# Wider fill beside the attention of a hybrid block, and four of its gates moved into the dense stage

## The chip, the cores and the metric

The kernel runs on one core of a Trainium2 chip. The metric is the device time of one execution in microseconds (us). A core has five engines with their own instruction queues: TensorE (PE, matrix products and transposes), VectorE (DVE), ScalarE (ACT), GpSimd (POOL) and SyncE (SP, which here only starts DMA transfers). They work side by side and wait for each other through semaphores. [...]

## The reference

One residual block over 1024 tokens with 1024 channels, all in float32. One input projection is divided among three token mixers and the gates; each mixer's output is projected, gated and summed; then comes a convolutional gated feed-forward network.

```python
h = _rmsnorm(x, norm_mix_g)
z = h @ w_in
(hq, hf, hi, hg, fq, fk, fv, ff, mq, gate_logits) = split(z)
y_a = _hgrn2_mixer(hq, hf, hi, hg, ...)  # recurrence, 4 heads, state 128 x 128; hi is its outcome (values)
y_b = _fox_mixer(fq, fk, fv, ff, ...)    # causal softmax attention, 8 heads x 64, with forget bias, q and k normed
y_c = _memory_mixer(mq, mem_kv, ...)     # attention into 256 memory tokens, 4 heads x 128
gates = sigmoid(gate_logits).reshape(B, T, 3, D_MODEL)
merged = sum(gates[:, :, i] * (y_i @ w_br_i) for i in range(3))
x = x + merged @ w_out
h2 = _rmsnorm(x, norm_ffn_g)
a, v = split(h2 @ w_up)                  # 2816 columns each
x = x + (gelu(causal_dwconv3(a)) * v) @ w_down
```

The forgetting attention ("fox") is, per head and block of 128 queries: scores q k^T / 8 plus a bias that depends on the key and the query, masked to the past, softmax over the keys, times v.

## The kernel before

**Arithmetic.** Every operand of a large product is kept as two rounded parts, high and low (`uh`, `ul` for the normed input, `wh`, `wl` for weights), and a product is three passes, high x high, high x low and low x high: `mm3`, L158 to L162, three matmul instructions for each block of 128 contraction rows. A split is a cast on ACT (or POOL) and a subtraction on DVE (`split`, L172 to L174). Weights are loaded to `raw` by SP and split into `wh` and `wl`, three buffers of each, shared by all stages up to the feed-forward one.

**Stages, in order of time.** (1) Input normalization, keys and values of the memory, two gates. (2) The dense stage: seven units (`dense_unit`, L628), each of which computes two chunks of 128 output channels over all tokens by a scheme of 7 products of half size in place of 8; the chunks are the 4 memory queries and `NPAIR = 10` gates. A gate is a tanh of the projected chunk, written to DRAM (`gd`) and read again in the branches. (3) Values and first projections of the fox attention, woven with the memory attention. (4) The fox attention, 8 heads, with fill beside it. (5) The HGRN recurrence, 4 heads (`hgrn_prep`, `hgrn_mix`). (6) The three branch products with their gates, (7) `w_out`, (8) the feed-forward network: up projection in units of the same scheme, then down.

**The fox attention.** Pair p holds heads 2p and 2p + 1. `fox_proj(p)` projects the pair's keys and queries: for each of 8 token blocks one PSUM tile `pp` of 256 columns with 8 x 3 matmuls, evacuated to `z` on ACT; after four blocks come squares on ACT (L859), a sum on DVE (L860), a power on POOL and a multiplication of `z` on DVE (L862). `fox_prep(p)` transposes `z` (L878, four transposes in one row of the profile's table: `x4`) and makes from each transposed tile `tr` the high and low parts `kh`, `kl` of the keys and both parts `qa` of the queries (ACT L883 and L889, DVE L884 and L890, POOL for copies). `fox_attn(p, i)` works on two query blocks at a time (`tp`, 4 times a head): score matmuls into `lg` (L924, L925: 512 keys wide at most, two matmuls each, two banks in all), a custom instruction on DVE that adds the bias, writes the logits `pt` to memory and keeps the maximum (L930), the exponential on ACT, the division on POOL; then it transposes the probabilities 128 x 128 at a time into `tr` (L953, L954), splits them into `ph` and `pl` (up to 512 wide) and multiplies by the values (`vhl`, a split of `Vf` by DVE) into `po`, 256 columns at a time (L965, L966). DVE evacuates `po` through `yp` (L970) to DRAM.

**What sets the order.** The program is written as generators; `weave` takes steps from several of them in proportion to their lengths. Steps inside `ahead` get a higher priority. A scheduler then fixes each engine's order by priority and by a model of time; `tc.issue_after(x)` holds an instruction behind `x` in that order. So an engine's queue is fixed when the chip starts. The fill beside attention is: `fox_proj(p + 1)` beside head 2p, `gates_early` (gates one at a time, 2 halves of 8 x 3 matmuls of 512 each) beside heads 1, 3, 5 and 6, and `hgrn_values`, the HGRN outcome in two parts of 256 columns, beside heads 6 and 7. None of it is tied to the attention's steps. The transposes of `fox_prep(p + 1)` are held behind the last score matmul of head 2p (`fox_sets[p][3]`).

Later places that the change touches: the first HGRN head is prepared by `hgrn_prep(0)` once the attention has ended; the tiles `yc` of the memory branch are loaded by POOL (L1311) after the last HGRN head's norm; the first feed-forward unit starts while `w_out`'s results are still being summed and normed, and calls `snap` (an ACT copy of a PSUM tile) after its second product, and `spread(r2, rt2)` (a broadcast of the norm's factors) after the casts of block T3.

## Time and profile before

| what | us |
|---|---|
| timed runs | 1698.60, 1698.73, 1700.01 (median 1698.73) |
| profiled execution, its own time | 1700.23 |
| span of that execution | 1698.4 |
| attention with its fill (stage 4), about | 325 to 680 |
| HGRN stage, about | 680 to 900 |
| first and last load of up weights | 1053 and 1437 |

The span is the part of the execution that the profile covers, from the first to the last instruction. In the profile a row of a group reads: line, engine, operation, tile written <- tiles read, shapes, count | busy us and mean ns of one | idle time of the engine just ahead of them and what ended it. A row of the timeline has the start in us, the duration, and in brackets the idle time before it with its releaser. A row of stretches has its bounds and length, then for PE, weight loads, DVE, ACT and POOL the busy us with the number of instructions, then the clock granted to PE, the DMA share and GB/s.

### The profile page before, as it was taken

How to read it: one execution, taken by the hardware profiler on the slowest of the kernel's cores; microseconds unless marked ns; L12 is line 12 of the kernel's file. 1: busy time of each engine (PE TensorE's matmuls, PEld its weight loads, DVE VectorE, ACT ScalarE, POOL GpSimd, SP SyncE). 2: the span in 40 equal slices, each digit the busy share in tenths (PEclk: the TensorE clock that was granted, in tenths of full speed). 3: DMA queues.
4: the chain of work that ended last, by engine and by line, in shares of the span. 5: the costliest groups of instructions: out<-in, count | busy, mean ns of one | idle time of the engine just before them, and what ended most of it. 6: DMA issues, size and time to landing. Idle time of an engine off the chain costs nothing.

```text
span 1698.4 us, 24291 instructions
## 1 busy us (share of the span) xinstructions
PE 1691.0 (100%) x8957; PEld 1452.4 (86%) x8957; DVE 1150.8 (68%) x2057; ACT 800.9 (47%) x1428; POOL 324.6 (19%) x420
## 2 busy tenths in 40 slices
...
GB/s 367 157 161 106 88 139 68 77 92 51 94 59 77 63 46 57 67 32 13 106 127 209 167 186 100 165 174 169 158 139 138 118 149 143 172 363 145 251 269 87
DMA packets 83062, 227.16 MB, mean 134 GB/s; under 512 B 9712, under 2 KB 12408, under 8 KB 82816
## 3 DMA queue, kind: packets, MB, share of 16 engines
...
q0 software_dynamic: 18048, 64.50, 13.2%
...
## 4 chain that ended last, share of the span: by engine, by line
PE 99%; DVE 0%; ACT 0%; DMA 0%; issue 0%; ACTq 0%; DVEq 0%
PE pp L160 21%; PE pp L162 21%; PE pp L161 21%; PE lg L160 4%; PE lg L162 4%; PE lg L161 4%; PE tr L162 3%; PE tr L161 3%; PE tr L160 3%; PE po L966 1%; PE lg L925 1%; PE lg L924 1%; PE po L965 1%; PE po L160 1%; PE po L161 1%; PE po L162 1%
## 5 line engine op out<-in xcount | busy, mean ns | idle before, releaser
L160 PE MATMUL pp<-uh,wh 128*128 128x512 f32 x412 | 163.3, 396 | 0.0
L161 PE MATMUL pp<-ul,wh 128*128 128x512 f32 x412 | 162.9, 395 | 0.0
L162 PE MATMUL pp<-uh,wl 128*128 128x512 f32 x412 | 162.5, 394 | 0.0
L161 PE MATMUL pp<-wl,uh 128*128 128x256 f32 (+1 forms) x512 | 146.3, 286 | 0.0
L162 PE MATMUL pp<-wh,ul 128*128 128x256 f32 (+1 forms) x512 | 146.1, 286 | 0.0
L160 PE MATMUL pp<-wh,uh 128*128 128x256 f32 (+1 forms) x512 | 145.6, 286 | 0.0
L166 ACT CAST wh<-s 128x512 fp32r<-128x512 f32 x110 | 66.5, 621 | 131.6 <-PE pp L161 55.1
L166 ACT CAST wh<-raw 128x1024 fp32r<-128x1024 f32 (+2 forms) x76 | 67.6, 890 | 100.6 <-PE pp L161 86.2
L166 ACT CAST wh<-rw 128x512 fp32r<-128x512 f32 x87 | 53.2, 619 | 108.1 <-PE pp L161 70.2
L160 PEld LDWEIGHTS pp<-wh,uh 128*128 128x128 f32 x512 | 97.3, 190 | 1.2
L161 PEld LDWEIGHTS pp<-wl,uh 128*128 128x128 f32 x512 | 97.4, 190 | 1.0
L162 PEld LDWEIGHTS pp<-wh,ul 128*128 128x128 f32 x512 | 97.4, 190 | 0.9
L1457 POOL DMA_DIRECT2D rw<-in_w_up x44 | 24.1, 555 | 372.4 <-DVE wl L1350 171.3
L166 ACT CAST dwh<-wr 128x1024 fp32r<-128x1024 f32 (+1 forms) x41 | 40.2, 980 | 115.8 <-PE tr L161 40.0
L162 PEld LDWEIGHTS pp<-uh,wl 128*128 128x128 f32 x412 | 77.5, 188 | 15.1
L174 DVE TENSOR_TENSOR wl<-raw,wh 128x1024 fp32r<-128x1024 f32 (+2 forms) x75 | 78.0, 1040 | 17.8 <-ACT wh L166 17.6
L160 PEld LDWEIGHTS pp<-uh,wh 128*128 128x128 f32 x412 | 77.5, 188 | 14.6
L161 PEld LDWEIGHTS pp<-ul,wh 128*128 128x128 f32 x412 | 77.5, 188 | 14.5
L940 ACT ACTIVATE pt<-pt,st 128x128 f32<-128x128 f32 (+3 forms) x64 | 49.7, 777 | 41.7 <-DVE st L937 33.9
L174 DVE TENSOR_TENSOR dwl<-wr,dwh 128x1024 fp32r<-128x1024 f32 (+1 forms) x41 | 46.3, 1129 | 31.7 <-ACT dwh L166 31.7
L942 POOL TENSOR_SCALAR pt<-pt,st 128x128 f32<-128x128 f32 (+3 forms) x64 | 49.1, 767 | 78.4 <-DVE st L941 64.1
L1350 DVE TENSOR_TENSOR wl<-rw,wh 128x512 fp32r<-128x512 f32 x69 | 47.7, 704 | 22.7 <-PE pp L162 18.2
...
## 6 DMA issues: line engine op xcount, KB each, us to landing
rw<-in_w_up POOLq DMA_DIRECT2D x44, 512.0 KB, 4.7
sd<-in_w_dn POOLq DMA_DIRECT2D x30, 512.0 KB, 6.0
br<-yd SPq DMA_DIRECT2D x30, 512.0 KB, 5.0
raw<-in_w_cm SPq DMA_DIRECT2D x24, 512.0 KB, 3.4
gd<-gt SPq DMA_DIRECT2D x48, 256.0 KB, 2.0
gt<-gd SPq DMA_DIRECT2D x48, 256.0 KB, 2.7
yd<-fc SPq DMA_DIRECT2D x44, 256.0 KB, 2.2
wr<-sd SPq DMA_DIRECT2D x20, 512.0 KB, 4.5
```

The costliest lines, as they stand in the source:

```text
L160: PE.matmul(ps, lh, rh, start=first, stop=False, skip_group_check=more)
L161: PE.matmul(ps, lh, rl, start=False, stop=False, skip_group_check=more)
L162: return PE.matmul(ps, ll, rh, start=False, stop=last, skip_group_check=more)
L166: return S.copy(out, in_)
L174: return (sub or V).tensor_sub(l, src, h.bitcast(F32))
L924: PE.matmul(ps[:, :w], qa[i][:, tsl], kh[i][:, s0:s0 + w], start=True, stop=False)
L925: fox_sets[p][3] = PE.matmul(ps[:, :w], qa[i][:, tsl], kl[i][:, s0:s0 + w], start=False, stop=True)
L940: S.activation(pt[:, :ns], pt[:, :ns], AF.Exp, bias=st[:, 2:3], accum_out=st[:, 3:4])
L942: G.tensor_scalar(pt[:, :ns], pt[:, :ns], st[:, 3:4], 0.0, ALU.mult, ALU.add)
L965: PE.matmul(o, vhl[:, sb, :], ph[:, src], start=(sb == 0), stop=False)
L1350: late["split"] = V.tensor_sub(l, src, h.bitcast(F32))
L1457: late["raw"] = G.dma_start(raw[:, 2 * i:2 * i + 2, :], src[:, 2 * i:2 * i + 2, :])
```

## The change

Four gates leave the fill of the attention and become two more units of the dense stage (`NPAIR` 10 to 14, 6 gates left beside the attention). The keys and queries of pairs 2 and 3 are projected together, 512 columns wide, by `fox_proj_late` into DRAM (`zd`), and read back, by `fox_load`, beside heads 2 and 3, where the squares and the norm are done in two halves of 8 groups. The HGRN outcome is projected 512 wide too, into DRAM (`hid`), and read back into `Vf` after the attention. The attention works on four query blocks at a time (two groups a head): four score steps, then for each key block up to four transposes into one `tr`, one split, and second products of 512, 384, 256 or 128 columns. Each query block has a tile `pt0` to `pt7` of its own. The list `at` records the last matmul of each step, and `paced` holds each chunk of fill behind the fourth last of them; the fill is dealt as 8 steps of pair 1's projection, 4 and 4 of the wide projection, then 4 a head of the gates and the outcome. The last output of the attention is evacuated in the midst of `hgrn_prep(0)`, whose seven steps are each held behind an earlier step of the attention. `yc` is loaded in eight parts within the first branch. Split weights have 4 buffers instead of 3. At the start of the feed-forward stage the raw weights of the unit that was begun ahead come by SP, the snapshot goes behind T3's casts and the broadcast behind product B22. The space for POOL's DMA descriptors is set to 2048 bytes.

```diff
-NCOVER, NPAIR = 2, 10
+NCOVER, NPAIR = 2, 14
...
-NFOX = [0, 3, 0, 3, 0, 3, 1]
+NFOX, NMID, NREST = 6, 0, (4, 4, 4, 4, 4)
-FOX_STEPS, HGRN_STEPS, MEM_STEPS = 28, 14, 7
+FOX_STEPS, HGRN_STEPS, MEM_STEPS = 22, 14, 7
...
-FOX_LATE = 0.2
+FOX_LAG = 4
+WIDE = 4
...
-            hl = [wp.tile([P, 4 * 264], F32R, tag=t, name=t, bufs=3) for t in ("wh", "wl")]
+            hl = [wp.tile([P, 4 * 264], F32R, tag=t, name=t, bufs=WIDE) for t in ("wh", "wl")]
...
+    zd = tc.dram_tile([8, P, HB], F32, name="zd")
+    def fox_norm(z):
+        zz = z.rearrange("p b (h d) -> p (b h) d", d=64)
+        r = cp.tile([P, 16], F32, tag="fr", name="fr", bufs=2)
+        for i in range(2):
+            sq = pq.tile([P, 8, 64], F32, tag="fsq", name="fsq")
+            S.activation(sq, zz[:, 8 * i:8 * i + 8, :], AF.Square)
+            V.reduce_sum(r[:, 8 * i:8 * i + 8], sq, axis=AX.X)
+        rstd_small(r, r, 64)
+        V.tensor_mul(zz, zz, r.unsqueeze(2).to_broadcast([P, 16, 64]))
+    def fox_tile(p, n):
+        fox_z.setdefault(p, {})[n] = z = pq.tile([P, 4, 256], F32, tag="z", name=f"z{p}_{n}", bufs=2)
+        return z
     def fox_proj(p):
...
+                fox_norm(z)
         yield from token_major(w_fqk[p], 256, evac)
+    def fox_proj_late():
+        def evac(tb, ps):
+            t = gate_tile()
+            S.activation(t, ps, AF.Copy, scale=rt[:, tb:tb + 1])
+            SP.dma_start(zd[tb], t)
+        yield from token_major(w_late[0], HB, evac)
+    def fox_load(p):
+        cs = slice((p - 2) * 256, (p - 1) * 256)
+        for n in range(2):
+            z = fox_tile(p, n)
+            SP.dma_start(z, zd[4 * n:4 * n + 4, :, cs].rearrange("b p c -> p b c"))
+            fox_norm(z)
+            yield
...
+    at = []
+    def paced(gen, lag):
+        while True:
+            with tc.issue_after(at[-lag].ins) if len(at) >= lag else nullcontext():
+                try:
+                    next(gen)
+                except StopIteration:
+                    return
+            yield
+    def fox_out(yp, po, dst):
+        S.copy(yp, po[64:128, :])
+        V.tensor_add(yp, po[0:64, :], yp)
+        SP.dma_start(dst, yp)
...
-        for tp in range(4):
+        for g in range(2):
...
+            for tb in range(4 * g, 4 * g + 4):
...
-                pt = pf.tile([P, T], F32, tag="pt", name="pt", bufs=4)
+                pt = pf.tile([P, ns], F32, tag=f"pt{tb}", name=f"pt{tb}")
...
                 pts.append(pt)
+                at.append(fox_sets[p][3])
                 yield
             po = ps_po()
-            for sp in range(tp + 1):
+            for sb in range(4 * g + 4):
                 ptr = ps_tr()
...
+                first = max(sb - 4 * g, 0)
+                for j in range(first, 4):
+                    PE.transpose(ptr[:, j * P:(j + 1) * P], pts[j][:, sb * P:(sb + 1) * P], ident)
                 ph = pf.tile([P, HB], F32R, tag="ph", name="ph", bufs=2)
                 pl = pf.tile([P, HB], F32R, tag="pl", name="pl", bufs=2)
...
+                c = slice(first * P, HB)
+                split(S, ph[:, c], pl[:, c], ptr[:, c])
+                PE.matmul(po[:, c], vhl[:, sb, :], ph[:, c], start=sb == 0, stop=False)
+                at.append(PE.matmul(po[:, c], vhl[:, sb, :], pl[:, c], start=False, stop=sb == 4 * g + 3))
                 yield
...
+            if (h, g) == (7, 1):
+                late["tail"] = po, ybd[a, p, g * HB:(g + 1) * HB]
+                return
+            fox_out(pf.tile([64, HB], F32, tag="yp", name="yp"), po, ybd[a, p, g * HB:(g + 1) * HB])
...
-    for p in range(3):
-        weave((ahead(fox_attn(p, 0), AHEAD), FOX_STEPS), (fox_proj(p + 1), 8))
-        fox_prep(p + 1, fox_sets[p][3])
-        weave((ahead(fox_attn(p, 1), AHEAD), FOX_STEPS), (gates_early(NFOX[2 * p + 1]), 2 * NFOX[2 * p + 1], FOX_LATE))
+    hid = tc.dram_tile([8, P, HB], F32, name="hid")
+    def hgrn_values():
+        def evac(tb, ps):
+            t = gate_tile()
+            S.activation(t, ps, AF.Copy, scale=rt[:, tb:tb + 1])
+            SP.dma_start(hid[tb], t)
+        yield from token_major(w_late[1], HB, evac)
+    late_proj = fox_proj_late()
+    values = hgrn_values()
+    rest = chain(gates_early(NFOX - NMID), values)
+    fill = [(fox_proj(1), 8), (chain(gates_early(NMID), islice(late_proj, 4)), 4 + 2 * NMID), (islice(late_proj, 4), 4)]
+    fill += [(islice(rest, n), n) for n in NREST]
+    for h in range(7):
+        p = h // 2
+        loads = {2: [(fox_load(2), 2, 0.9)], 3: [(fox_load(3), 2, 0.1)]}.get(h, [])
+        gen, n = fill[h]
+        weave((ahead(fox_attn(p, h % 2), AHEAD), FOX_STEPS), (paced(gen, FOX_LAG), n), *loads)
+        if h % 2 == 0 and p < 3:
+            fox_prep(p + 1, fox_sets[p][3])
+    run_all(late_proj)
...
-    for h in (6, 7):
-        fox_vsplit(h)
-    values = hgrn_values()
-    for i in range(2):
-        weave((ahead(fox_attn(3, i), AHEAD), FOX_STEPS), (islice(values, 8), 8),
-              (gates_early(0 if i else NFOX[6]), 2 * NFOX[6], FOX_LATE))
+    weave((ahead(fox_attn(3, 1), AHEAD), FOX_STEPS), (paced(fill[7][0], FOX_LAG), fill[7][1]))
     run_all(values)
+    for tb in range(8):
+        SP.dma_start(Vf[:, tb, :], hid[tb])
...
-    run_all(hgrn_prep(0))
+    tail = hgrn_prep(0)
+    for i, lag in enumerate((12, 9, 6, 3, 1, 1, 1)):
+        run_all(paced(islice(tail, 1), lag))
+        if i == 2:
+            fox_out(gate_tile()[:64, :], *late.pop("tail"))
...
+    first_branch = branch(0, yh, yl)
     yc = [[py.tile([P, T], F32R, tag=f"yc{p}{c}", name=f"yc{p}{c}") for c in range(4)] for p in "hl"]
-    for c in range(4):
-        for t, d in zip(yc, ycd):
-            with tc.issue_after(state["norm"].ins):
-                G.dma_start(t[c], d[:, c, :].bitcast(F32R))
-    run_all(branch(0, yh, yl))
+    for i, _ in enumerate(first_branch):
+        if i % 3 and i < 12:
+            p, c = i % 3 - 1, i // 3
+            mark = G.tensor_scalar(warm, late["gates"][:, 0:1], 1.0, 0.0, ALU.mult, ALU.add)
+            with tc.issue_after(mark.ins):
+                G.dma_start(yc[p][c], ycd[p][:, c, :].bitcast(F32R))
     run_all(branch(2, *yc))
...
+            with tc.issue_after(late["pow"].ins) if after else nullcontext():
+                late["raw"] = (SP if begun else G).dma_start(raw[:, 2 * i:2 * i + 2, :], src[:, 2 * i:2 * i + 2, :])
...
-        product(y, o4, "B22", False)
+        ins = product(y, o4, "B22", False)
+        if begun:
+            e2 = late["e2"]
+            with tc.issue_after(ins.ins):
+                spread(r2, rt2)
         put(0, 1, y, e2)
...
             if name == "T3":
-                spread(r2, rt2)
+                with tc.issue_after(late["cast"].ins):
+                    late["e2"] = snap(late.pop("x"))
...
-    nc = bacc.Bacc("TRN2", target_bir_lowering=False, num_devices=1)
+    nc = bacc.Bacc("TRN2", target_bir_lowering=False, num_devices=1, dynamic_dma_scratch_size=2048)
```

Two places show how the engines' orders move. The first is TensorE at the start of head 4 (pair 2, i = 0), where the second half of `fox_prep(2)` is transposed (`z2_1`, by `ident`, into `tr`). Before (`pp` is fill, the projection of pair 3):

```order
L160 MATMUL pp_5399<-wh_5254,uh0_79 128x256
L161 MATMUL pp_5399<-wl_5255,uh0_79 128x256
L878 MATMUL tr_4749<-ident_72,z2_1_4542 128x128 x4
L162 MATMUL pp_5399<-wh_5254,ul0_80 128x256
L160 MATMUL pp_5399<-wh_5254,uh1_81 128x256
L878 MATMUL tr_4762<-ident_72,z2_1_4542 128x128 x4
L161 MATMUL pp_5399<-wl_5255,uh1_81 128x256
L162 MATMUL pp_5399<-wh_5254,ul1_82 128x256
```

And with the change (`pp_4994` is a gate, `lg` the scores of head 4, the last five rows transposes of the probabilities of head 3):

```order
L163 MATMUL pp_4994<-uh7_93,wl_4889 128x512
L967 MATMUL lg_5286<-kh0_2_4819,qa0_2_4821 128x128
L967 MATMUL lg_5333<-kh0_2_4819,qa0_2_4821 128x256
L968 MATMUL lg_5286<-kl0_2_4823,qa0_2_4821 128x128
L968 MATMUL lg_5333<-kl0_2_4823,qa0_2_4821 128x256
L905 MATMUL tr_4847<-ident_72,z2_1_4803 128x128 x4
L905 MATMUL tr_4860<-ident_72,z2_1_4803 128x128 x4
L994 MATMUL tr_4973<-ident_72,pt0_4874 128x128
L994 MATMUL tr_4973<-ident_72,pt1_4921 128x128
L994 MATMUL tr_4973<-ident_72,pt2_4934 128x128
L994 MATMUL tr_4973<-ident_72,pt3_4959 128x128
L994 MATMUL tr_4984<-ident_72,pt1_4921 128x128
```

Before, fill stands between the transposes; now the first row is the last fill until 36 rows later, and the first scores of the new head and head 3's probabilities follow.

VectorE at the same place, before:

```order
L464 TENSOR_TENSOR gt_5231<-pp_5206,rx_95 128x512
L174 TENSOR_TENSOR wl_5869<-raw_5866,wh_5868 128x1024
L970 TENSOR_TENSOR yp_4658<-po_4580,yp_4658 64x256
L174 TENSOR_TENSOR vhl_5235<-Vf_1789,vhl_5235 128x8x64
L884 SCALAR_TENSOR_TENSOR kl0_2_4725<-tr_4727,cv_71,kh0_2_4721 64x512
L890 SCALAR_TENSOR_TENSOR qa0_2_4723<-tr_4740,fqs_185,qa0_2_4723 64x512
L884 SCALAR_TENSOR_TENSOR kl1_2_4726<-tr_4727,cv_71,kh1_2_4722 64x512
L890 SCALAR_TENSOR_TENSOR qa1_2_4724<-tr_4740,fqs_185,qa1_2_4724 64x512
```

And with the change (`fr` and `fsq` belong to the norm of pair 3's keys and queries, read back from DRAM; `gt` is the evacuation of a gate):

```order
L917 SCALAR_TENSOR_TENSOR qa1_2_4822<-tr_4838,fqs_185,qa1_2_4822 64x512
L465 TENSOR_TENSOR gt_5019<-pp_4994,rx_95 128x512
L175 TENSOR_TENSOR wl_5731<-raw_5728,wh_5730 128x1024
L855 TENSOR_REDUCE fr_4949<-fsq_4950 128x8
L911 SCALAR_TENSOR_TENSOR kl0_2_4823<-tr_4847,cv_71,kh0_2_4819 64x512
L917 SCALAR_TENSOR_TENSOR qa0_2_4821<-tr_4860,fqs_185,qa0_2_4821 64x512
L855 TENSOR_REDUCE fr_4949<-fsq_4953 128x8
L911 SCALAR_TENSOR_TENSOR kl1_2_4824<-tr_4847,cv_71,kh1_2_4820 64x512
L179 TENSOR_SCALAR fr_4949<-fr_4949 128x16
L917 SCALAR_TENSOR_TENSOR qa1_2_4822<-tr_4860,fqs_185,qa1_2_4822 64x512
L855 TENSOR_REDUCE fr_5151<-fsq_5152 128x8
L973 ISA pt0_5282,st_5283<-lg_5286,nfm_5284 128x128
```

The evacuation of the gate, a split of weights and the norm of pair 3 now stand among the preparations of pair 2, ahead of the first score reduction of head 4 (the last row, "ISA"; L930 before).

The second place is TensorE at the start of head 6 (pair 3), with the change:

```order
L163 MATMUL pp_5824<-uh7_93,wl_5731 128x512
L967 MATMUL lg_6104<-kh0_3_5661,qa0_3_5663 128x128
L968 MATMUL lg_6104<-kl0_3_5665,qa0_3_5663 128x128
L905 MATMUL tr_5689<-ident_72,z3_1_5149 128x128 x4
L967 MATMUL lg_6168<-kh0_3_5661,qa0_3_5663 128x256
L968 MATMUL lg_6168<-kl0_3_5665,qa0_3_5663 128x256
L905 MATMUL tr_5702<-ident_72,z3_1_5149 128x128 x4
L994 MATMUL tr_5803<-ident_72,pt0_5716 128x128
```

Here too the fill (first row) ends ahead of the new pair's last transposes and the first scores of its first head.

84 lines of the change are left out of this document (27 added, 57 removed).

## The prediction

> **What bounds the kernel now.** I read the page first, for who is busy and what the chain of waits is made of.
>
> ```profile
> span 1698.4 us, 24291 instructions
> PE 1691.0 (100%) x8957; PEld 1452.4 (86%) x8957; DVE 1150.8 (68%) x2057; ACT 800.9 (47%) x1428; POOL 324.6 (19%) x420
> PE 99%; DVE 0%; ACT 0%; DMA 0%; issue 0%; ACTq 0%; DVEq 0%
> ```
>
> TensorE (PE) never stops and is 99% of the chain. So time is PE's instructions times their spacing, plus whatever waits the change opens. A busy PE may still be slow, so the second view is the table of stretches, and the third the timeline of PE, where the spacing is the distance from one start to the next and not the printed duration (matmuls overlap).
>
> ```profile
> 325.00:680.00 355.00, 355.00 (x2351) 324.44 (x2350) 216.46 (x648) 179.93 (x352) 122.56 (x172) 1.00 0.19 65
> 1300.00:1400.00 100.00, 100.00 (x443) 82.80 (x442) 78.73 (x117) 41.91 (x64) 14.01 (x23) 1.00 0.45 133
> 205.63 0.28 PE L160 MATMUL pp<-wh,uh 128*128 128x256 f32 x1
> 205.75 0.28 PE L161 MATMUL pp<-wl,uh 128*128 128x256 f32 x1
> 205.87 0.28 PE L162 MATMUL pp<-wh,ul 128*128 128x256 f32 x1
> 339.12 0.22 PE L965 MATMUL po<-ph,vhl 128*128 128x128 f32 x1
> 339.18 0.28 PE L966 MATMUL po<-pl,vhl 128*128 128x128 f32 x1
> 339.29 0.30 PE L953 MATMUL tr<-ident,pt 128*128 128x128 f32 x1
> 559.95 0.60 PE L878 MATMUL tr<-ident,z 128*128 128x128 f32 x4
> 560.31 0.48 PE L924 MATMUL lg<-kh,qa 128*128 128x512 f32 x1
> ```
>
> Columns of the first two rows: busy us and count of PE, weight loads, VectorE (DVE), ScalarE (ACT), GpSimd (POOL). From them: a 512-wide matmul takes 100/443 = 0.226 us, a 256-wide one 0.12, a pair of 128-wide ones 0.06 + 0.11 = 0.17, a transpose 0.36/4 = 0.09; a 384-wide one I put midway, 0.173. In the attention stretch (first row) PE is covered throughout, DVE is busy 61%, ACT 51%.
>
> **The change, part by part: what PE no longer does.** (a) Four gates leave the stage beside the attention and become two more units of the dense stage. Alone each has 2 halves x 8 blocks x 3 passes = 48 matmuls of 512; a unit has 7 products x 4 x 3 = 84 for two gates. So 192 become 168: 24 x 0.226 = 5.4 us off. (b) The projections of head pairs 2 and 3 and the outcome (HGRN values) go from 256 to 512 columns: 768 matmuls at 0.12 (92.2 us) become 384 at 0.226 (86.8): 5.4 off. (c) The second product of the attention goes from 320 matmuls (256 of 256 columns, 64 of 128) to 192 (96 of 512, 32 each of 384, 256, 128): 30.7 + 32 x 0.17 = 36.1 against 21.7 + 5.5 + 3.8 + 2.7 = 33.7: 2.4 off. The transposes stay 288. (d) By these spacings the attention's PE work of before comes to 340 us, where the first row above has 355: 4% go at changes of width. The stage now holds about 65 us less, so up to 2.6 less of that; I take 2.0. Sum 15.2, ends 13.2 and 15.8.
>
> [...]
>
> (e) One wait of before stands in the groups:
>
> ```profile
> L1189 PE MATMUL po<-St,qe 128*128 128x128 f32 x56 | 11.1, 280 | 0.8 <-DVE St L1195 0.7
> ```
>
> It sits in the last HGRN head, whose order moves; worth 0 to 0.7, I take 0.5 off. (f) At the start of the feed-forward stage a snapshot is put behind the casts of T3 and the spread of the second norm behind product B22. One copy of 128x512 moves; PE waits nearly nothing there now. I take +0.3, ends -0.2 and +2.
>
> **What PE must wait for.** Every part above leaves PE less to do beside the attention while DVE's and ACT's work there stays: the same reductions, exponentials and splits. The fill (projections and gates) used to be free to run at any time; now each chunk is held behind the fourth-last step of the attention, and in the order of the change the fill is missing at the four places where the next pair's keys and queries are prepared and a new head starts. What runs there on DVE:
>
> ```profile
> L884 DVE SCALAR_TENSOR_TENSOR kl<-tr,cv,kh 64x512 fp32r<-64x512 f32 x16 | 12.0, 750 | 7.3 <-ACT kh L883 7.1
> L890 DVE SCALAR_TENSOR_TENSOR qa<-tr,fqs,qa 64x512 fp32r<-64x512 f32 x16 | 12.0, 750 | 3.1 <-ACT qa L889 2.6
> L862 DVE TENSOR_TENSOR z<-z,fr 128x1024 f32<-128x1024 f32 x8 | 11.5, 1438 | 1.6 <-POOL fr L179 1.5
> L860 DVE TENSOR_REDUCE fr<-fsq 128x16 f32<-128x1024 f32 x8 | 9.7, 1216 | 2.6 <-ACT fsq L859 2.6
> L174 DVE TENSOR_TENSOR wl<-raw,wh 128x1024 fp32r<-128x1024 f32 x46 | 57.0, 1239 | 15.3 <-ACT wh L166 15.2
> L174 DVE TENSOR_TENSOR pl<-tr,ph 128x512 fp32r<-128x512 f32 x48 | 32.2, 684 | 12.0 <-ACT ph L166 11.8
> L174 DVE TENSOR_TENSOR pl<-tr,ph 128x384 fp32r<-128x384 f32 x32 | 17.6, 549 | 1.4 <-ACT ph L166 1.3
> L174 DVE TENSOR_TENSOR vhl<-Vf,vhl 128x512 fp32r<-128x512 f32 x8 | 5.4, 676 | 0.0
> L464 DVE TENSOR_TENSOR gt<-pp,rx 128x512 f32<-128x512 f32 x24 | 16.3, 687 | 20.3 <-PE pp L162 20.3
> L930 DVE CUSTOM_DVE_ANT_0 pt<-lg,nf 128x384 f32<-128x384 f32 x16 | 8.8, 552 | 1.5 <-PE lg L925 1.4
> L930 DVE CUSTOM_DVE_ANT_0 pt<-lg,nf 128x256 f32<-128x256 f32 x16 | 6.7, 418 | 5.4 <-PE tr L953 4.0 <-PE lg L925 1.3
> L930 DVE CUSTOM_DVE_ANT_0 pt<-lg,nfm 128x128 f32<-128x128 f32 x64 | 18.2, 285 | 13.2 <-POOL nfm L919 7.0 <-PE lg L925 2.8 <-PE po L965 2.0
> 429.79 0.69 DVE L930 CUSTOM_DVE_ANT_0 pt<-lg,nf 128x512 f32<-128x512 f32 x1 [2.34 <-PE tr L953]
> 430.40 0.41 DVE L970 TENSOR_TENSOR yp<-po,yp 64x256 f32<-64x256 f32 x1
> 430.74 0.27 DVE L930 CUSTOM_DVE_ANT_0 pt<-lg,nfm 128x128 f32<-128x128 f32 x1
> ```
>
> The last three rows show that back to back an instruction holds DVE for 0.08 us less than its duration (0.69 to 0.61, 0.41 to 0.34), and that a reduction's readout adds nothing. So I take each mean less 0.08.
>
> The worst place is the start of head 4. Between the last score matmul of head 3 (which DVE needs before it goes on) and the fourth row block of head 4 (whose bank DVE must have emptied), PE has 24 fill matmuls, 25 transposes, 6 narrower score and 5 second-product matmuls: 5.4 + 2.3 + 0.8 + 0.9 = 9.4 us. DVE has, in order, 8 kl and qa (5.4), 2 multiplications of z (2.7), 4 half reductions (half of 1.216, less 0.08: 2.1), one weight split (1.2), a gate (0.6), vhl (0.6), yp at twice its width (0.6, from 0.676 and 0.750 of like shapes), two pl (1.1), score reductions 0.5 + 0.3 + 4 x 0.2 (1.6), and seven narrow ones (about 1.3): 17.2 us. So PE stands some 7.8 us. Counted alike: head 6, 8.1 on DVE against 4.3 on PE (3.9); head 0, 17.9 against 15.5 (2.4); head 2, 13.4 against 11.6 (1.8). Together 15.9. The same reckoning over the order of before finds no place in the attention, and one of 0.9 at L1189, where the row above has 0.7: it errs little.
>
> This counts DVE as never waiting. In the rows of kl and qa it waited 7.3 + 3.1 us for ACT's half of the work in four preparations; all of that on top gives 26. The lower end is three quarters, 12, as at L1189. I take 20, nearer the count, because DVE hides part of these waits behind its other rows.
>
> Sum: -15.2 - 0.5 + 0.3 + 20 = +4.6. The profiled execution took 1700.23 us (its span of 1698.4 and 1.8 around it), so it would take 1704.8; the three timed runs have a median of 1698.73, 1.5 less, and with the same difference I get **1703** us. Costed at nothing: 28 further DRAM transfers on SP's queue (z and the outcome go out in 8 tiles each and come back in 4 and 8) hidden by heads of some 35 us each; POOL's share, busy 35% in the stretch; the fourth buffer of split weights. Without that cover the copies cost what the fourth rival says.
>
> **The rivals.** First, DVE keeps up: it enters each place with its queue empty and the waits shrink to some 4 us in all; then 1698.7 - 15.7 + 4.3 = 1687. For it: DVE is busy only 61% of the stretch. Against: the first instruction of each of the four chains needs a matmul of that place, so an empty queue does not help. Second, savings and waits cancel (13 to 18 us of waits): 1695 to 1702, no change; the bare count of 15.9 points there.
>
> Third, slower by more: the waits trip the clock.
>
> ```profile
> 4.00:7.30 3.30, 1.51 (x8) 0.95 (x8) 1.75 (x7) 2.29 (x5) 0.00 (x0) 1.00 1.07 387
> 7.30:10.70 3.40, 3.40 (x10) 2.62 (x9) 2.73 (x6) 1.95 (x6) 0.00 (x0) 0.50 1.00 393
> ```
>
> After a stretch of 3.3 us in which PE worked 1.51, the granted clock (third from the right) was 0.50 for 3.4 us. At head 4 PE works 9.4 of 17 us, at head 6 4.3 of 8. Each such window costs up to 1.7 us; five of them 8: 1711. [...] Against: all later slices had the full clock, and part of the loss would fall into waits. [...]
>
> Fourth, the copies come late: the squares of z stand in ACT's queue ahead of exponentials, and a late z holds all of them. From the issues:
>
> ```profile
> br<-yd SPq DMA_DIRECT2D x30, 512.0 KB, 5.0
> gd<-gt SPq DMA_DIRECT2D x48, 256.0 KB, 2.0
> rw<-in_w_up POOLq DMA_DIRECT2D x44, 512.0 KB, 4.7
> sd<-in_w_dn POOLq DMA_DIRECT2D x30, 512.0 KB, 6.0
> L1457 POOL DMA_DIRECT2D rw<-in_w_up x44: 527/559/582, 1053.3 to 1437.0; - x44
> ```
>
> 2.0 out and 5.0 back is 7 us per tile if nothing covers it; one of the four uncovered gives 1709. Against: pair 3's copy is not needed for two heads. The smaller space for POOL's descriptors I cost at nothing: even one load at a time, those of w_up and w_dn take 44 x 4.7 + 30 x 6.0 = 387 us, and their issues are spread over 384 (last row).
>
> **How the numbers follow.** Forecast 0.34, cancel 0.22, DVE keeps up 0.25, clock 0.11, late copies 0.08. A measurement of this kernel tells about 0.2% (3.4 us) from no change: slower (over 1702.1) 0.53, the same 0.22, faster 0.25. The likeliest case alone spans 1702 to 1709; with the ends of waits (12 to 26) and the neighbours, half of the case in which DVE keeps up among them, 1685 to 1712 holds 8 in 10.
>
> **What would show it.** PE's own matmuls must come to some 15 us less, with two more dense units. Idle PE released by DVE must stand in the rows of score matmuls and transposes of the attention, at four places, the longest at the start of head 4 just after fill chunks of the gates; DVE must be packed there. Wrong would be: PE idle under 5 us in the whole attention (then near 1687), waits named DMA or ACT there, or a granted clock of 0.5 in the middle of the run.

## The result, and the profile after

| | before | after |
|---|---|---|
| timed runs, median (lowest to highest), us | 1700.01 (1698.60 to 1700.32, 5 runs) | 1729.47 (1728.52 to 1730.77, 5 runs) |
| profiled execution: own time, span, mean granted clock | 1700.23, 1698.4, 0.999 | 1729.44, 1727.6, 0.993 |
| PE idle in the span (span less PE's busy time), us | 7.4 | 31.4 |

The ratio of the times is 1.0177, with a 95% interval of 1.0162 to 1.0192. The prediction was 1703 with a range of 1685 to 1712: the direction was right, the size was not, and the time lies outside the range.

The first rows of the page of after: the span, the busy time of each engine, and the chain of waits.

```profile
span 1727.6 us, 23268 instructions
PE 1696.2 (98%) x8421; PEld 1426.9 (83%) x8421; DVE 1162.3 (67%) x2089; ACT 802.6 (46%) x1436; POOL 333.5 (19%) x430
PE 93%; DVE 3%; DMA 1%; ACT 1%; issue 1%; POOL 0%; ACTq 0%; SPq 0%; DVEq 0%; POOLq 0%
```

PE has 536 matmuls fewer, and yet its busy time is 5 us longer (at half clock a 512-wide matmul keeps PE for 0.43 us, from 423.70 to 424.12 and on, against 0.23 at full clock, from 429.45 on). The chain has lost 6% of PE; half of that went to DVE. Next the table of stretches of after: first the attention in three pieces, then the stretches of 10 us in which something happens, then two later stages. The columns are those of before; the two to look at are PE's busy us (first) and its granted clock (third from the right).

```profile
330.00:500.00 170.00, 156.72 (x934) 136.84 (x933) 114.42 (x337) 97.05 (x194) 79.88 (x102) 0.97 0.24 79
500.00:600.00 100.00, 90.58 (x450) 74.43 (x451) 66.98 (x205) 50.91 (x105) 43.66 (x57) 0.93 0.22 73
600.00:690.00 90.00, 89.76 (x453) 74.85 (x452) 43.53 (x134) 39.32 (x74) 20.53 (x28) 1.00 0.29 99
...
360.00:370.00 10.00, 6.49 (x33) 6.25 (x34) 9.19 (x24) 5.38 (x11) 9.21 (x15) 0.71 0.07 25
410.00:420.00 10.00, 6.97 (x37) 5.76 (x35) 7.32 (x15) 4.86 (x9) 7.43 (x11) 1.00 0.33 116
420.00:430.00 10.00, 8.18 (x41) 6.97 (x42) 8.19 (x31) 7.04 (x17) 5.74 (x11) 0.83 0.01 3
490.00:500.00 10.00, 8.23 (x44) 6.45 (x42) 9.74 (x22) 7.54 (x12) 8.93 (x9) 1.00 0.47 146
500.00:510.00 10.00, 5.32 (x19) 3.88 (x20) 9.78 (x27) 6.00 (x13) 9.00 (x9) 0.66 0.43 131
580.00:590.00 10.00, 6.17 (x21) 4.63 (x21) 7.99 (x24) 5.82 (x14) 7.10 (x11) 0.66 0.22 79
...
690.00:910.00 220.00, 220.00 (x1244) 185.84 (x1243) 151.53 (x254) 122.59 (x301) 74.56 (x63) 1.00 0.18 59
1090.00:1690.00 600.00, 598.06 (x2652) 494.74 (x2651) 453.58 (x622) 254.79 (x361) 68.54 (x105) 1.00 0.59 184
```

PE stands at four places, and the clock falls at each of them: near 360, 420, 500 and 580. The HGRN stage stays full (second last row), and the feed-forward stage has 1.94 us idle (last row), where before had 0.2. The groups of PE with the longest waits say who is late:

```profile
L994 PE MATMUL tr<-ident,pt 128*128 128x128 f32 x288 | 49.1, 286 | 14.3 <-DVE kl L911 13.9 <-DVE pl L175 0.2 <-DVE qa L917 0.2
L905 PE MATMUL tr<-ident,z 128*128 128x128 f32 x64 | 9.4, 275 | 2.8 <-DVE z L857 2.3 <-DVE qa L917 0.6
L967 PE MATMUL lg<-kh,qa 128*128 128x512 f32 x48 | 20.3, 423 | 1.7 <-DVE st L973 1.5
L161 PE MATMUL tr<-B21h,wh 128*128 128x512 f32 x88 | 34.4, 390 | 0.8 <-ACT r L369 0.8
L162 PE MATMUL tr<-B21l,wh 128*128 128x512 f32 x88 | 34.3, 390 | 0.8 <-DVE B21l L175 0.8
```

And the timeline of PE has the single waits, in the last bracket; between the rows before 497 and at 503 lies the start of head 4:

```profile
361.47 0.63 PE L905 MATMUL tr<-ident,z 128*128 128x128 f32 x4 [2.27 <-DVE z L857]
365.15 0.69 PE L967 MATMUL lg<-kh,qa 128*128 128x384 f32 x1 [2.04 <-DVE st L973]
421.60 0.63 PE L994 MATMUL tr<-ident,pt 128*128 128x128 f32 x4 [4.63 <-DVE kl L911]
496.00 0.39 PE L163 MATMUL pp<-uh,wl 128*128 128x512 f32 x1
497.10 0.60 PE L905 MATMUL tr<-ident,z 128*128 128x128 f32 x4
498.26 0.63 PE L905 MATMUL tr<-ident,z 128*128 128x128 f32 x4 [0.56 <-DVE qa L917]
503.72 1.87 PE L994 MATMUL tr<-ident,pt 128*128 128x128 f32 x7 [4.84 <-DVE kl L911]
509.50 0.50 PE L967 MATMUL lg<-kh,qa 128*128 128x512 f32 x1 [0.91 <-DVE st L973]
583.83 1.73 PE L994 MATMUL tr<-ident,pt 128*128 128x128 f32 x7 [4.44 <-DVE kl L911]
```

The last fill matmul (`pp`, at 496.00) is just ahead of the transposes of `z`, so the chunk of fill is used up before the wait begins. Behind it DVE works without a break; its timeline in that time:

```profile
498.14 0.69 DVE L465 TENSOR_TENSOR gt<-pp,rx 128x512 f32<-128x512 f32 x1
498.75 1.29 DVE L175 TENSOR_TENSOR wl<-raw,wh 128x1024 fp32r<-128x1024 f32 x1
499.96 0.67 DVE L855 TENSOR_REDUCE fr<-fsq 128x8 f32<-128x512 f32 x1
500.56 0.73 DVE L911 SCALAR_TENSOR_TENSOR kl<-tr,cv,kh 64x512 fp32r<-64x512 f32 x1
501.32 0.74 DVE L917 SCALAR_TENSOR_TENSOR qa<-tr,fqs,qa 64x512 fp32r<-64x512 f32 x1
502.10 0.69 DVE L855 TENSOR_REDUCE fr<-fsq 128x8 f32<-128x512 f32 x1
502.82 0.76 DVE L911 SCALAR_TENSOR_TENSOR kl<-tr,cv,kh 64x512 fp32r<-64x512 f32 x1
```

The transposes of the probabilities use the same two `tr` banks (the two buffers the kernel has for `tr`) as those of `z`, so they wait for the `kl` at 502.82, and that stands in DVE's queue behind a gate, a weight split and two reductions. The place and the order of DVE are those of the prediction.

**Where the 29 us are.** By the first three rows of the stretches PE idles 13.3, 9.4 and 0.2 us (22.9 together, none before the change), by the last one 1.9 in the feed-forward stage. The granted clock was 0.5 from 364.1, 500.7 and 582.6 on for 6.83 us each and from 422.2 on for 3.41. PE is busy 5.8, 3.8, 5.6 and 3.3 us of these, 18.4 together. Counted as half at full clock, that work loses some 9.2 us. This is an estimate and rather an upper end: a 512-wide matmul takes 0.43 us there and 0.23 at full clock, a 256-wide one 0.21 (from 365.96 on) and 0.12 (at 371.37), and by these pairs 18.4 us lose 8 to 8.6. The rest comes from the matmuls one by one: each lasts to the start of the next or to its own end, whichever is first, half of what lies at half clock is taken off, and the times are added by what the operands belong to. The line (c), (d) holds the attention's own matmuls.

| term | predicted, us | measured, us |
|---|---|---|
| (a), (b) fill: gates to the dense stage, wide projections | -10.8 | -10.6 |
| (c), (d) second product, changes of width | -4.4 | +6.0 |
| (e) wait at L1189 and near it | -0.5 | -0.8 |
| (f) start of the feed-forward stage | +0.3 | +2.3 |
| waits in the attention | +20 | +22.9 |
| half clock behind them | 0 (a rival) | about +9.2 |
| all else | 0 | +0.1 |
| sum | +4.6 | +29.1 of 29.2 |

Line (a), (b): the fill and the dense stage together have 408 matmuls fewer (3468 to 3060). Line (c), (d): the attention's own matmuls took 105.5 us before and 111.6 after. At the usual distance for each width (its median in before) they would take 100.2 and 98.3. The rest is 4.2 us in after for the ends of 21 matmuls just ahead of a wait, which belong to the waits, and gaps too short to show as idle time, 5.3 before and 9.1 after; 3.2 us of that growth lie in the second product.

### The profile page after: what moved, and what is told of

Same layout as the page of the kernel before. It is cut to its first block, busy times and chain, and to the rows that moved or that the text cites. A ratio compares the mean times of both kernels' runs of the same rounds, so it can differ in the third digit from the quotient of the medians.

```text
span 1727.6 us, 23268 instructions
## 1 busy us (share of the span) xinstructions
PE 1696.2 (98%) x8421; PEld 1426.9 (83%) x8421; DVE 1162.3 (67%) x2089; ACT 802.6 (46%) x1436; POOL 333.5 (19%) x430
## 4 chain that ended last, share of the span: by engine, by line
PE 93%; DVE 3%; DMA 1%; ACT 1%; issue 1%; POOL 0%; ACTq 0%; SPq 0%; DVEq 0%; POOLq 0%
PE pp L161 20%; PE pp L162 20%; PE pp L163 20%; PE lg L161 5%; PE lg L163 5%; PE lg L162 5%; PE tr L161 3%; PE tr L162 3%; PE tr L163 3%; PE tr L994 2%; PE po L1000 1%; PE po L161 1%; PE po L162 1%; PE po L163 1%; PE po L999 1%; PE lg L1200 1%
## 5 line engine op out<-in xcount | busy, mean ns | idle before, releaser
L162 PE MATMUL pp<-ul,wh 128*128 128x512 f32 x356 | 140.4, 394 | 0.0
L162 PE MATMUL pp<-wl,uh 128*128 128x256 f32 (+2 forms) x384 | 125.0, 326 | 0.0
L161 PE MATMUL pp<-wh,uh 128*128 128x256 f32 (+2 forms) x384 | 124.8, 326 | 0.0
L163 PE MATMUL pp<-wh,ul 128*128 128x256 f32 (+2 forms) x384 | 123.9, 323 | 0.0
L175 DVE TENSOR_TENSOR wl<-raw,wh 128x1024 fp32r<-128x1024 f32 (+2 forms) x71 | 72.5, 1021 | 13.3 <-ACT wh L167 13.2
L163 PEld LDWEIGHTS pp<-wh,ul 128*128 128x128 f32 x384 | 73.8, 192 | 5.2
L161 PEld LDWEIGHTS pp<-wh,uh 128*128 128x128 f32 x384 | 73.9, 192 | 5.1
L163 PEld LDWEIGHTS pp<-uh,wl 128*128 128x128 f32 x356 | 66.9, 188 | 13.4
L162 PEld LDWEIGHTS pp<-ul,wh 128*128 128x128 f32 x356 | 66.9, 188 | 13.3
L162 PEld LDWEIGHTS pp<-wl,uh 128*128 128x128 f32 x384 | 73.9, 193 | 4.6
L167 ACT CAST ph<-tr 128x512 fp32r<-128x512 f32 (+1 forms) x96 | 44.2, 479 | 64.5 <-PE tr L994 55.2
L973 DVE CUSTOM_DVE_ANT_0 pt<-lg,nf 128x512 f32<-128x512 f32 (+2 forms) x80 | 41.2, 526 | 41.9 <-PE tr L994 22.2
L175 DVE TENSOR_TENSOR pl<-tr,ph 128x512 fp32r<-128x512 f32 (+1 forms) x96 | 51.9, 552 | 21.6 <-ACT ph L167 21.3
```

The source lines that it names most:

```text
L161: PE.matmul(ps, lh, rh, start=first, stop=False, skip_group_check=more)
L162: PE.matmul(ps, lh, rl, start=False, stop=False, skip_group_check=more)
L163: return PE.matmul(ps, ll, rh, start=False, stop=last, skip_group_check=more)
L167: return S.copy(out, in_)
L175: return (sub or V).tensor_sub(l, src, h.bitcast(F32))
L973: V.tensor_tensor_reduce(out=pt[:, s0 + lo:s0 + hi], in0=ps[:, lo:hi], in1=bias, op0=ALU.add, op1=ALU.max, scale=1.0, scalar=-3e38, accum_ ...
```

## Experiments

Theory A: PE waits where the attention's own matmuls hang on a chain of DVE instructions and no other work of PE stands behind them in its queue. What was taken from beside the attention was that other work, and the half clock follows from the waits. All runs below start from the changed kernel unless the kernel before is named; "idle" is the span less PE's busy time, 7.4 in before and 31.4 in after; the clock is the mean granted one, 0.999 and 0.993.

### Useless work behind the transposes

```diff
+DULL_COVER = 8, 18, 18, 18
...
+        with tc.high_priority(AHEAD), tc.issue_after(turned.ins):
+            ps = ps_proj()
+            for _ in range(DULL_COVER[p]):
+                PE.matmul(ps, uh[0][:, :P], ul[0][:, :HB], start=True, stop=True)
```

The added products are read by nothing.

> Extra matmuls whose result nobody reads (8 at the preparation of pair 0, 18 at those of pairs 1, 2 and 3, 512 wide, 62 x 0.227 = 14 us of work) are put behind the last transposes of each pair's keys and queries, so that TensorE has something to do while VectorE drains. Theory A (TensorE stands for 24 us at four places and each stand then halves the granted clock for some 7 us, which costs another 10): idle time at the four places falls below 10 us, the granted clock stays 1.00 through the attention, and although 14 us of useless work are added the time falls by 6 to 10 us, to some 1720. Rival B (the low clock has another cause than the stands, or costs nothing): the clock still falls at the same places, and the time stays at 1729 or rises by up to 4.

Measured: 1761.09 us (1760.18 to 1761.16), idle 48.0, clock 0.988. A miss. The table of waits of PE (who waits for whom: us in total, times, longest) shows why:

```profile
PE tr L906 <- DVE z L858: 18.4, 3, 8.3
PE lg L972 <- DVE qa L918: 14.5, 3, 5.7
```

The 13.9 us for `kl` are gone, so these waits were covered; but in the new order the real chunks stand behind the useless ones, and the wait went one step ahead, to `z` itself, and grew. The order is the scheduler's, and an insertion moves everything near it. The run neither supports nor refutes A.

### The fill let free

```diff
-FOX_LAG = 4
+FOX_LAG = 1000
```

> The fill beside the attention is no longer held behind the fourth last step of the attention (the paced tail behind the attention loses its holds too). Theory A (the fill is missing at the places where keys and queries are prepared): fill comes early and covers the first places, but there is no more of it, so it runs out and the idle time comes back at the last place and in the last heads: between 1715 and 1735, idle time in the attention 10 to 30 us. Rival C (holding the fill is the whole cause): idle time in the attention falls under 5 us and the time to some 1696 (1729 less 24 and 10).

Measured: 1723.11 us (1721.72 to 1724.81), idle 27.1, clock 0.992. Stretches of this run:

```profile
500.00:570.00 70.00, 70.00 (x354) 58.73 (x353) 39.32 (x102) 32.64 (x60) 23.91 (x29) 1.00 0.25 87
570.00:600.00 30.00, 27.45 (x141) 22.31 (x140) 20.40 (x69) 16.93 (x35) 11.40 (x16) 1.00 0.33 108
600.00:650.00 50.00, 36.62 (x174) 27.76 (x175) 38.97 (x145) 29.82 (x64) 24.13 (x41) 0.80 0.27 84
```

Free fill covers the first three places completely (PE is full from 330 to 570) and is then used up: the last heads stand bare, PE idles 13.4 of 50 us, and the clock falls to 0.80. The same DVE chains are there with and without waits, so the waits depend on where fill stands. That is A. Between this run and the change, the holding only chooses between waits late and waits early.

### The holding at another distance

```diff
-FOX_LAG = 4
+FOX_LAG = 28
```

> One number of the changed kernel: each chunk of fill is held behind the 28th last step of the attention instead of the 4th last, about one head earlier. In TensorE's order 43, 34, 28 and 28 matmuls of 512 columns (or as much) then stand between the two halves of the preparation at the four places, and 21, 36, 37 and 28 right behind the second half, where the changed kernel has 24, 33, 24, 26 and 12, 0, 0, 0. Theory A (fill is missing at the places, and each stand brings the low clock): the idle time of 24 us falls under 8 and the clock stays near 1.00 there; what is taken early is missing in the last heads, so some 5 us come back: 1729 - 16 - 8 + 5 = 1710 (1703 to 1717). Theory F (VectorE bounds the stage; cover only moves the waits): over 1720.

Measured: 1711.23 us (1708.25 to 1713.99), ratio to before 1.0066 (1.0050 to 1.0081), idle 19.1, clock 0.995. The time is as expected, and 18 us below the change from one number; the idle time in the attention is 10.5 us and not under 8, and two stretches of half clock are left. The group that waited 14.3 us:

```profile
L994 PE MATMUL tr<-ident,pt 128*128 128x128 f32 x288 | 50.0, 287 | 2.7 <-DVE pl L175 2.7
```

The long waits for `kl` are gone; short ones for `pl`, `st` and `yp` take their place.

### Gates put back beside the attention

Three runs: all four gates back with the fill held, all four with the fill free, two with the fill free.

```diff
-NCOVER, NPAIR = 2, 14
-NFOX, NMID, NREST = 6, 0, (4, 4, 4, 4, 4)
+NCOVER, NPAIR = 2, 10
+NFOX, NMID, NREST = 10, 0, (6, 6, 6, 5, 5)
```

> The four gates go back beside the attention (10 gates there, dealt 6, 6, 6, 5, 5 steps a head; five pairs less two in the dense stage), everything else as in the changed kernel. That adds 5.4 us of matmuls. Rival D (the stage has too little fill in all): idle time at all four places goes and the time falls to some 1701 (1729 + 5 - 24 - 10). Theory A (not how much but where): the first three places still wait 5 to 7 us each with the clock at half behind them, the fourth, where the order has fill behind the transposes, goes: 1729 + 5 - 8 = 1726.

Measured: 1726.72 us (1725.79 to 1727.59), idle 26.9, clock 0.994. As A expects; rival D falls. Giving back 43 us of fill hardly helps: the stands of heads 2 and 4 are unchanged (`L994` still waits 9.5 us for `kl` in two waits, 4.8 at the longest), and only that of head 6 is mostly gone. So with the fill held, where it stands matters more than how much there is.

> Both at once: ten gates beside the attention, and no holds on the fill. Theory A: with fill at all places and enough of it to the end, the idle time in the attention goes (under 5 us) and the clock stays at 1.00: from the run without holds (1723) less its 16 us idle and 10 us of low clock at the bare end, plus 5.4 us of matmuls, 1702 (1697 to 1707), the same as before the change. Theory F: waits of over 10 us remain, 1712 and more.

Measured: 1712.46 us (1711.53 to 1712.81), idle 17.9, clock 0.996, where I had expected 1702; the time is the one that F gave, the waits are a little shorter. No waits until 600; about 9 us of idle time and two stretches of half clock remain in the last heads, which are bare even with four gates more. What I had missed is that free fill runs ahead of the heads it is dealt to, as in the run before, however much of it there is.

> Two of the four gates back beside the attention (eight there), no holds on the fill. The run without holds was bare from 594 to 676 us; two gates are 21.8 us of TensorE work more there and cost 2.7 us of matmuls. Theory A: the bare end shortens by a third to a half, its 26 us with it: 1723 + 2.7 - 10 = 1716 (1709 to 1720). If fill had to be complete at every place, the time would fall all the way, to some 1700.

Measured: 1717.09 us (1715.89 to 1718.31), idle 20.7, clock 0.994. As expected. With free fill the time goes 1723, 1717, 1712 for 0, 2 and 4 gates back, although each pair put back costs 2.7 us of extra matmuls: so each pair is worth some 8 us as cover (an estimate from these three times).

### Is it the ring of `tr` banks, the copies, or a late norm?

Three runs change the order inside one place. First, the preparation of the next pair is emitted after the eighth step of the following head.

```diff
+PREP_AT = 8
...
+                for i, _ in enumerate(steps):
+                    if i == PREP_AT:
+                        fox_prep(p + 1, last)
```

> The keys and queries of pairs 1 to 3 are prepared in the program behind the eighth step of the following head in place of ahead of that head, so that the transposed tiles of the head's first group no longer stand behind theirs in the ring of two banks. Theory E (the ring is what makes TensorE wait: a head's second products cannot start before the next pair's late keys have been taken out of the two banks): idle time at the places of pairs 1 to 3 falls by two thirds and the time to some 1708. Theory A: something must cover VectorE's work wherever the preparation stands: idle time stays over 15 us, the time 1722 to 1732.

Measured: 1729.48 us (1727.94 to 1731.55), idle 29.2, clock 0.993. The waits of `L994` for `kl` shrink from 13.9 to 2.0 us, and others grow to nearly the same sum (20.6 us in the attention, 22.9 in the change); PE's table of waits:

```profile
PE po L1000 <- ACT ph L168: 5.1, 4, 2.1
PE lg L968 <- DVE st L974: 4.5, 6, 2.0
PE lg L968 <- DVE qa L918: 4.2, 2, 2.2
PE tr L995 <- DVE kl L912: 2.0, 3, 1.5
```

The name of the wait changes, the time does not: the shared `tr` banks decide which instruction is seen to wait, not how long PE is without work.

Second and third, pair 3's copy and norm are moved to head 4, in the program only, and then behind head 4's exponentials.

```diff
-        loads = {2: [(fox_load(2), 2, 0.9)], 3: [(fox_load(3), 2, 0.1)]}.get(h, [])
+        loads = {2: [(fox_load(2), 2, 0.9)], 4: [(fox_load(3), 2, 0.1)]}.get(h, [])
```

> The keys and queries of pair 3 are read back and normed beside head 4 in place of head 3, so that their squares, sums and multiplications no longer stand in VectorE's queue at the place where pair 2 is prepared. Theory A with a packed VectorE: the waits at that place (7.3 us with the narrow ones) fall by the 1.3 us of sums ahead of the awaited row, and by up to 1.5 behind it, the time by 2 to 5 us, to some 1725. Rival G (these norms are what makes VectorE late): the wait there goes (under 1.5 us) and with it the low clock, 1729 less 9 = 1720.

Measured: 1731.93 us (1730.79 to 1735.76), idle 30.1, clock 0.992. The order of the engines did not change at the place, so this run tells nothing about the norm.

```diff
-        loads = {2: [(fox_load(2), 2, 0.9)], 3: [(fox_load(3), 2, 0.1)]}.get(h, [])
+        loads = {2: [(fox_load(2), 2, 0.9)], 4: [(behind_exp(fox_load(3)), 2, 0.3)]}.get(h, [])
```

Here `behind_exp` holds each step behind the last exponential of the attention.

> The norm of pair 3's keys and queries is really moved now: its squares stand in ScalarE's queue behind an exponential of head 4, so its sums and multiplications leave VectorE's queue at the place where pair 2 is prepared (run e6 changed the program but not the order). At that place the changed kernel waits 0.8 + 5.0 + 1.2 us. Theory A with a packed VectorE: two sums (1.3 us) and ScalarE's squares ahead of the awaited row go, so the 5.0 fall to 3.0 to 3.7, and the 1.2 go; with less low clock 3 to 5 us in all: 1725. Rival G (these norms make VectorE late there): the wait falls under 1.5 us, 1720 or less. Rival I (the wait is a chain of single steps of ScalarE and VectorE, not a queue): it stays within 0.5 us of 5.0.

Measured: 1731.70 us (1729.32 to 1732.70), idle 30.4, clock 0.991. The group that waits for `kl`:

```profile
L1003 PE MATMUL tr<-ident,pt 128*128 128x128 f32 x288 | 49.8, 289 | 13.2 <-DVE kl L911 12.8 <-DVE pl L175 0.2 <-DVE qa L917 0.2
```

At the start of head 4 the wait for `kl` falls from 4.84 to 3.53 us, inside the 3.0 to 3.7 that A gave and about what two half reductions off a packed DVE give (2 x 0.6), so rivals G and I fall. The time does not fall, against the 1725 expected: 1.6 us of waits and a half clock of 3.4 us appear at 544, where the norm now stands, and the half clock at head 0 lasts 10.2 us in place of 6.8.

### Fill set by hand at the four places

```diff
+    def covered(cover, count, after):
+        for _ in range(count):
+            with tc.high_priority(AHEAD), tc.issue_after(after.ins):
+                if next(cover, 1) == 1:
+                    return
+            late["covered"] = late["chunk"]
...
-            fox_prep(p + 1, fox_sets[p][3])
+            fox_prep(p + 1, fox_sets[p][3], islice(rest if p else late_proj, 2))
```

Two whole chunks of fill are taken from the deal of the heads and placed at each preparation.

> The same fill, dealt otherwise: at each of the four places two of its chunks are set by hand, one between the transposes of the first and the second half of a pair's keys and queries, one right behind the second half, both ahead in priority; the heads get 5, 3, 3, 4, 2, 4, 3 and 3 chunks beside them. Theory A (VectorE is late there and TensorE needs work that does not hang on it): idle time in the attention falls from 24 us to under 6, the granted clock stays at 1.00, and the time falls by 24 + 10 less what is left, to some 1698 (1694 to 1704). Theory F (VectorE bounds the attention stage as a whole, so cover at one point is missed at another): the waits come back between the places and the time stays over 1715.

Measured: 1723.77 us (1721.64 to 1726.95), idle 30.0, clock 0.996. The long waits for `kl` are gone and others have come: 5.2 us for `kh` (POOL's copy) at 355, 5.8 in score matmuls, 3.3 and 2.9 around the second products. The time is the one that F gave. A chunk is 24 matmuls, 5.4 us in one lump; given to one place it is missing elsewhere. The half clock lasts 13.7 us in place of 23.9, and the work in it loses, by the same count, 6.1 us in place of 9.2: 3 of the 6 us gained.

### The start of the feed-forward stage put back

```diff
-                    late["e2"] = snap(late.pop("x"))
+                spread(r2, rt2)
...
-                late["raw"] = (SP if begun else G).dma_start(raw[:, 2 * i:2 * i + 2, :], src[:, 2 * i:2 * i + 2, :])
+                late["raw"] = G.dma_start(raw[:, 2 * i:2 * i + 2, :], src[:, 2 * i:2 * i + 2, :])
```

> The start of the feed-forward stage is put back as it was: raw weights by GpSimd, the snapshot after its product, the broadcast behind the casts of T3. Theory: the wait of some 2.5 us at 1105 to 1112 us goes, time 2 to 3 us less than the changed kernel, 1727. Rival: the wait belongs to something else and the time does not move.

Measured: 1734.41 us (1733.87 to 1734.61), idle 33.7. A miss in sign: from its first product to PE's last matmul the stage takes 639.4 us without the edit, 635.0 with it (and 632.7 in before). The edit is a gain of about 4 in the new surroundings; the stage is still 2.3 us longer than before, of which the rows of `tr<-B21h` and `tr<-B21l` above wait 1.6.

### Each part of the change by itself

Two query blocks at a time in the changed kernel:

```diff
-        for g in range(2):
+        for tp in range(4):
...
-            for sb in range(4 * g + 4):
+            for sp in range(tp + 1):
```

> The attention works on two query blocks at a time again, with second products of 256 columns (2.4 us more matmuls); the fill, its holds and the wide projections stay. Theory A (missing fill): the four places still wait for VectorE, the time stays within 1722 to 1735. Rival H (four score steps in a row ahead of the second products are what overloads VectorE): idle time in the attention under 8 us and a time of some 1705.

Measured: 1739.26 us (1738.63 to 1741.27), idle 33.6, clock 0.988. Ten us slower than the change, and above the range that A gave; rival H falls. The wide attention is not what costs inside the change: it gains there.

Three runs then take one part each. The gates alone, in the kernel before:

```diff
-NCOVER, NPAIR = 2, 10
+NCOVER, NPAIR = 2, 14
...
-NFOX = [0, 3, 0, 3, 0, 3, 1]
+NFOX = [0, 2, 0, 2, 0, 2, 0]
```

> The kernel before with one part of the change alone: four gates move from beside the attention into the dense stage (14 there; 2, 2 and 2 beside heads 1, 3 and 5), with the old attention, the old narrow projections and no holding of the fill. Simple sum: 24 matmuls of 0.226 us fewer, 1700.2 - 5.4 = 1695. Theory A (the cover that leaves beside the attention is what opens the waits): the stage loses 192 matmuls or 43 us of TensorE work, heads 6 and 7 keep only the outcome's projection, and idle TensorE of 10 to 18 us released by DVE or ACT stands in the attention, with some windows of half clock behind it: 1705 to 1715, I say 1711. If A is right and this part carries the loss, it stands above 1705; at 1695 the gates are innocent.

Measured: 1718.23 us (1716.73 to 1718.71), ratio 1.0107 (1.0092 to 1.0122), idle 21.4, clock 0.998. Five us of matmuls are saved and the time is still 18 us longer, above the 1705 to 1715 that A gave. Of the idle time 8.2 us stand in the attention (A gave 10 to 18) and 4.5 in the HGRN stage behind it. By the count used above, the attention's own matmuls, whose instructions are those of before, take 5.7 us more (3.5 of them ends ahead of waits, 2.0 short gaps). The longest wait of the attention is in a late head; the worst stretch of the attention:

```profile
600.00:610.00 10.00, 6.70 (x42) 4.89 (x40) 7.56 (x36) 6.33 (x14) 3.91 (x7) 1.00 0.19 67
```

The four-block attention, in the kernel before, with the smaller space for POOL's descriptors (not in the lines below):

```diff
-        for tp in range(4):
+        for g in range(2):
...
-            for sp in range(tp + 1):
+            for sb in range(4 * g + 4):
```

> The kernel before with only the four-block attention (two groups a head, second products up to 512 wide, one evacuation a group) and the smaller space for POOL's descriptors; gates, projections and their order as before. Simple sum: 2.4 us fewer in second products and up to 0.5 of width changes, 1700.2 - 2.9 = 1697. Rival K (the four-block attention carries the loss, since it makes longer chains on DVE and its second products wait for their splits): 1715 or more with more than 15 us idle in the attention. Theory A: the cover is all there, so waits stay under 10 us in the attention, 1700 to 1709, I say 1705.

Measured: 1721.42 us (1720.87 to 1723.03), ratio 1.0129 (1.0114 to 1.0144), idle 24.8, clock 0.996. The total is that of rival K, but not its mechanism, which asked for 15 us idle in the attention: there it is 2.3, as A has it, and the attention's own matmuls take 0.7 us less than before. The rest stands behind the attention, where neither theory looked: PE idles 3.0 us at its end, 4.0 in the first HGRN head and 8.0 in the first branch product. DVE's timeline there, two rows of PE's table of waits, and two rows of SP's timeline:

```profile
921.30 0.69 DVE L1282 SCALAR_TENSOR_TENSOR gt<-gt,pp 128x512 f32<-128x512 f32 x1 [11.38 <-DMA gt<-gd]
```

```profile
PE pp L160 <- DVE gt L1282: 8.0, 1, 8.0
PE tr L1163 <- DVE kE L1155: 4.0, 1, 4.0
```

```profile
902.77 6.06 SPq L1325 DMA_DIRECT2D x<-in_xT  x8
911.18 0.33 SPq L1275 DMA_DIRECT2D gt<-gd  x1
```

A gate read from DRAM kept DVE waiting 11.4 us; PE stood 8.0 us. POOL had asked for the eight tiles `yc` (512 KB each) at once from 894.5 on, but so it does in before, from 885.1 on, where DVE waits 1.8 us in all. What differs is in SP's queue: the eight loads of the residual `x` (512 KB each), which before are issued at 977, stand at 902.8 here, ahead of the awaited gate, whose load was issued at 911.18 and took 10.1 us (2.7 in the median). In before the same row is:

```profile
L1336 SPq DMA_DIRECT2D x<-in_xT x8: 327/422/666, 977.2 to 980.7; - x8
```

So this wait is again one of order, moved by an edit far ahead of it; whether the descriptor space has a share was not separated. The wait for `kE` is in the first HGRN head, begun only when the attention has ended. Neither wait is in the trace of the change, which begins `hgrn_prep(0)` early and issues the loads of `x` at 1003.7.

The wide projections and the edits of the later stages alone: the kernel of the two-block run above, with

```diff
-NCOVER, NPAIR = 2, 14
-NFOX, NMID, NREST = 6, 0, (4, 4, 4, 4, 4)
-FOX_LAG = 4
+NCOVER, NPAIR = 2, 10
+NFOX, NMID, NREST = 10, 0, (6, 6, 6, 5, 5)
+FOX_LAG = 1000
```

> The change with the attention on two query blocks at a time, ten gates beside it and no holding of the fill, so that the wide projections through DRAM and the edits of the later stages (yc in parts, the start of the feed-forward stage, which alone was worth about 4 us) are what is left of it. Simple sum: -5.4 - 4 = 1691. Theory A: beside the attention only 5.4 us of cover are missing, but the fill is dealt otherwise, pair 1's projection beside head 0 alone and the wide ones in chunks of 5.4 us beside heads 1 and 2, so places without fill remain at the end: 1700 to 1712, I say 1706. If the wide projections carry the loss, it stands above 1715.

Measured: 1721.09 us (1719.92 to 1722.56), ratio 1.0126 (1.0111 to 1.0141), idle 20.6, clock 0.996. That is above the 1700 to 1712 that A gave, and above the 1715 from which the wide projections were to carry the loss. But the fill is also dealt otherwise here: only 5.4 us of cover are gone, and still the last heads are bare:

```profile
620.00:630.00 10.00, 7.42 (x27) 5.88 (x27) 3.76 (x18) 3.28 (x9) 3.35 (x7) 0.50 0.18 66
```

This run is that with four gates back and free fill (1712.46), but with two query blocks at a time: there too the four-block attention gains, 8.6 us, as it gained 9.8 in the change.

So no one part carries the loss: taken alone they cost 18, 21 and 21 us, and all together 29. Each saves matmuls and opens waits of its own, and they do not add up: most of what the four-block attention cost alone stood behind the attention, in waits that the change does not have.

### Finer fill

Each chunk of fill is cut into eight pieces of three matmuls, dealt one by one. First with two of the four gates put back and a distance of 28 steps, then with none put back and a distance of 20.

```diff
+FINE = 8
+FOX_LAG = (28, 28, 28, 28, 28, 28, 28, 28)
...
+                if fine and k + 1 < KC and (k + 1) % 1 == 0:
+                    yield
...
-    fill += [(islice(rest, n), n) for n in NREST]
+    fill += [(islice(rest, n * FINE), n * FINE) for n in NREST]
```

> The change with two more gates beside the attention (8, and 12 in the dense stage), each chunk of fill cut into eight pieces of three matmuls that are dealt one by one, and each held behind the 28th step back. Theory A: fill is there at every place and none of it comes in a lump ahead of a wait, so TensorE's idle time in the attention falls under 12 us and hardly any window of half clock is left; the work saved is 2.7 us less than in the change: 1700 to 1708, I say 1704, against 1711 with whole chunks at the same lag. Rival F (the waits only move, since DVE's own work in the stage sets a floor for each head): 1710 or more, with the idle time as long as with whole chunks (15 us in all).

Measured: 1707.50 us (1705.37 to 1709.44), ratio 1.0045 (1.0029 to 1.0062), idle 16.8, clock 0.996. PE's longest wait in the attention:

```profile
PE tr L1002 <- DVE kl L919: 3.9, 1, 3.9
```

One long wait for `kl` is left (3.9 us at 419) and two stretches of half clock, of about 3.4 us each; from 330 to 690 PE idles 7.7 us, against 22.9 in the change. As A expects, at the upper end of what it gave (of the half clock more is left than it said); F, by which the waits only move, falls.

> The change with its 14 gates in the dense stage, each chunk of fill cut into eight pieces of three matmuls, held behind the 20th step back and dealt 4, 3, 3, 3 and 4 chunks to heads 3 to 7, the copies of pair 3 read beside head 4. Theory A: compared with the same fineness at 12 gates (1707.5) 2.7 us of TensorE work are saved, but 96 matmuls or 22 us of cover are gone from beside the attention too, so the idle time grows by about what is saved or more: 1706 to 1714, I say 1709, with the longest waits at the starts of heads where the fill has run out. Rival M (fineness alone was the cure, the amount of cover does not matter): 1702 to 1705, idle time as in the run with 12 gates.

Measured: 1714.57 us (1713.00 to 1714.99), ratio 1.0086 (1.0069 to 1.0103), idle 20.8, clock 0.995. Seven us slower than with two gates more beside the attention, although PE has 12 matmuls less, and 0.6 above the range that A gave; rival M falls. Fineness alone is not the cure. That the amount of cover counts too fits A, but this run also differs from the last in the distance, in the deal and in where pair 3 is read, so it does not show the amount by itself; the three runs with free fill above come closer to that.

No version tried was faster than the kernel before. The nearest is that with fine fill and 12 gates in the dense stage, 0.45% slower.

## Why the prediction was right or wrong

**What bounds, and the fill taken away.** Right. PE sets the time, and terms (a) and (b) came to 10.6 us of the 10.8.

**The waits.** Right in place and releaser, and short in size: four places, nearly all waits named DVE, in the transposes and score matmuls (1.3 us, at 470 and 481, are for ACT and in the second product), 22.9 us of idle time against 20 with ends of 12 and 26. With the ends of the matmuls ahead of them (4.2 us) they cost 27, just above the upper end. By place, forecast count and measured: head 4 7.8 and about 6.5 (0.56, 4.84 and 0.91 and small ones); head 6 3.9 and 4.4; head 2 1.8 and 4.8 (4.63 and 0.16); head 0 2.4 and about 5 (2.27, 2.04 and 0.56). That the sum came so near has some luck in it: head 4 was counted 1.3 us too long, and heads 0 and 2 together 5.6 too short. The count of DVE against PE was good where fill was counted in the right place, and too small at heads 0 and 2, where DVE also waited for its inputs (1.4 us for ACT's half of the keys at 357, 1.4 and 1.1 for ACT just ahead of 418 and 419). The rival in which DVE keeps up falls.

**The step that failed: the clock was made a rival instead of a term.** The prediction had one case of it, at the start of before: 1.51 us of PE work in 3.3 us, a share of 0.46, and 3.4 us at half clock behind it. Its own count had "PE works 9.4 of 17 us" at head 4, "at head 6 4.3 of 8", and since that work lies at the ends of the place, a stretch of 3.4 us inside it holds a smaller share than that, by the numbers of the forecast itself. In after the 3.41 us ahead of the four half clocks had shares of 0.48, 0.16, 0.31 and 0.06. The rival was still weighed at 0.11, for two reasons. That "all later slices had the full clock" said nothing, since before had no wait there. That "part of the loss would fall into waits" is true, but of the 23.9 us at half clock PE worked 18.4. As a consequence of the waits the clock belonged into the sum, where it was put at nothing, with the 8 us that the rival gave it: 1711 as the forecast, and a range that reaches some 8 us higher. The estimate from the trace is about 9.2. That alone would not have reached 1729: of the 24.6 us that the sum was short, the clock is 9, the waits (with the ends ahead of them) are 7, terms (c) and (d) 6 and (f) 2. The 9.2 us are an estimate from a count in the trace; no run kept the waits and took the half clock away.

**(c) right, (d) mis-sized by 6 us.** The prediction took the widths of the second product for 2.4 us off, and the changes of width for 2.0 off, in proportion to the work that leaves. At the usual distances the attention's own matmuls did fall by 2.0. But the short gaps between them, which (d) let shrink with the fill, grew by 3.7 us. Little of that is the price of the four-block form: with that form and the fill of before (the four-block run) these gaps take 6.2 us, with that form and fine fill at 12 gates 4.9, and with the old form and four gates taken away (the run with the gates alone) 7.4; before has 5.3 and the change 9.1. So most of the growth goes with the missing fill: PE's short waits, most of them at the second product, stand where fill stood between the steps.

**(e)** is right. **(f)** came to 2.3, just above the upper end of 2: 1.6 of it are the waits in `tr<-B21h` (for the broadcast `r`) and `tr<-B21l`. Yet undoing the edit was worse by 4, so its price in the order of before was the wrong question: what it replaces in the new order costs more.

**Late copies.** The mechanism is there, the price is not. No wait of PE in the attention is released by a DMA in the trace of after, but ACT waits 5.8 us, in three waits, for copies of `z`, as this rival said: one of them (1.17 us, up to 498.44) stands in ACT's queue at the start of head 4, ahead of the keys that PE then waits for. With that copy moved behind an exponential of head 4, the wait for `kl` fell by 1.3 us and the time did not fall, so the copies do not decide. The four-block run shows that transfers could have decided elsewhere, in the first branch product. No wait in these traces is named by the fourth buffer or the space for descriptors; they were not tried alone.

**What stays open.** Whether a deal of the fill exists that keeps the saved work and covers all places. Fine pieces came nearest; DVE's chains at the starts of heads 2 and 4 were still longer than what was left to cover them.
